# Weight units behind the last factors, and a first product between the two last of one bank, in a two-layer streaming encoder

## The chip, the cores and the metric

The kernel runs on one core of a Trainium2 chip. Its time is the device time of one execution in microseconds. A core has TensorE (PE; its weight loads are shown apart as PEld), VectorE (DVE), ScalarE (ACT), GpSimd (POOL) and SyncE (SP), which issues transfers. Each engine works through its own queue of instructions in order, and semaphores tie the queues together. Before the change three runs took 1084.51 to 1087.21 us, with a median of 1086.31.

## The reference

One step of an encoder with two layers, over 512 new frames of one stream and 64 of a running one, 576 columns together. Layer 0 mixes the frames by pooling, layer 1 by attention over selected keys. Behind each mixer stands a squared-ReLU MLP of 1024 to 4096 to 1024:

```python
def _mlp(h, w_up, w_down):
    u = jax.nn.relu(h @ w_up)
    return (u * u) @ w_down

for i in range(DEPTH):
    h = _rmsnorm(x, norm_mix[i])
    ...
    x = x + y.astype(x.dtype)
    x = x + _mlp(_rmsnorm(x, norm_mlp[i]), mlp_w_up[i], mlp_w_down[i]).astype(x.dtype)
return (_rmsnorm(x, norm_final), ...)
```

## The kernel before

**Numbers.** A float32 product is made of three products of a shorter format: every operand is split into a high part (a cast) and a low part (the rest). For weights this is a *unit*: L181 on ScalarE casts a raw 128x512 tile to `wh`, L182 on VectorE subtracts to get `wl`. For activations L470 on ScalarE and L473 on VectorE do the same, into `u`.

**Seven products.** In the MLP a block of two by two tiles is multiplied with seven products in place of eight (Strassen). `seven()` runs one such task. It uses three PSUM banks, `a`, `b` and `c`, and takes seven factors in this order: b11 into `b`, t1 into `c`, t2 into `b`, b21 into `a`, t3 into `b`, b22 into `c`, t4 into `b`. Behind the first product ScalarE copies `b` to `a` (L530). Each product is 12 matmuls of 128x288 (L501): four rows of the inner dimension, three matmuls each (wh with u's high part, wh with its low part, wl with the high part). Some weight units are sums of tiles, made on VectorE (L260, L264) from tiles that transfers have loaded and added to.

**Tasks.** An MLP is four chunks c of the inner width. Chunk 0 takes its up projection with plain products (L305). In c = 1, 2, 3, four up tasks `Up(c, j)` make four rows of activations (`u`, in L501's rows as `u_...`), then four down tasks `Down(q)` multiply them with the down weights and add to the residual x (L559). The fourth up task (j = 3) is *final*: its row is the last that the down tasks need. The first down task behind it is *late*: it runs rows 0 to 2 of its products first and row 3 behind them. This place is called a border here. There are six, at about 186, 277, 369, 834, 926 and 1017 us of the profiled execution.

**The final row.** An up task reads its banks with `lo0`, `hi1`, `hi0` and `lo1` while its last products still run. `hi1` adds a copy kept from bank `c` (`snap`) to bank `b` (L609), behind t3 and ahead of t4, which goes on to add into the same bank. L592 takes the ReLU times the norm's factor, L451 squares; L481, L484, L485 and L488 form the differences for t1, t2, t3 and t4 (the tile v, index 2, 3, 1, 0); `parts_of` splits them. In the last border of layer 1 the row's b12 part is also parked in PSUM (L494) and split later (L292) for the program's end.

**Order.** Nothing of this order is written by hand: a scheduler of the framework simulates the program and sets each engine's queue from the data's dependencies and its own estimates, in the order of the program where it has no reason for another. `ahead()` makes the next weight units, up to five ahead (`LEAD`), at the places where it is called, so the casts, subtractions and sums of later weights stand between the operations of the row. A raw tile is free for the next load (L213, on SyncE) once its unit is made, and GpSimd's queue adds a second tile to some of them in flight (L217, L238).

Of the kernel before, what the change touches and what calls it, by code (L numbers as in the profile page):

```python
# [12 lines left out]
ALU = mybir.AluOpType  # L13
# [9 lines left out]
HT = T // 2  # L23
# [33 lines left out]
def pool_dsa_kernel(ctx: ExitStack, tc: tile.TileContext, a, o):  # L57
    nc = tc.nc
    act, dve, pool, pe = nc.scalar, nc.vector, nc.gpsimd, nc.tensor
# [48 lines left out]
    def psum1(s="po"):  # L108
        return phase["po"].tile([P, 512], F32, tag="po", name=uid(s))

    def f32(t):
        return t.bitcast(F32)
# [156 lines left out]
    units = made()  # L269
# [18 lines left out]
    def split(dst, src, scale=None, sub=dve):  # L288

        if scale is None:  # L290
            act.copy(dst[:, 0], src)
            sub.tensor_tensor(dst[:, 1], src, f32(dst[:, 0]), ALU.subtract)  # L292
        else:
            act.activation(dst[:, 0], src, AF.Copy, scale=scale)
            dve.scalar_tensor_tensor(dst[:, 1], src, scale, f32(dst[:, 0]), ALU.mult, ALU.subtract)
# [101 lines left out]
    def mlp(layer, gi, late=0, end=None):  # L397
# [19 lines left out]
        parked = []  # L417
        rows = (0, 1, 2, 3)
# [48 lines left out]
                    phase["u"].tile([P, 7, 2, HT], F32R, tag="u", bufs=4, name=uid("u")))  # L467

        def upper(u, v, f):
            act.copy(u[:, f, 0], v[:, f])  # L470

        def lower(u, v, f):
            dve.tensor_tensor(u[:, f, 1], v[:, f], f32(u[:, f, 0]), ALU.subtract)  # L473

        def parts_of(u, v, f):

            upper(u, v, f)
            lower(u, v, f)

        def first_sum(v):  # L480
            dve.tensor_tensor(v[:, 2], v[:, 4], v[:, 1], ALU.subtract)  # L481

        def middle_sums(v):
            dve.scalar_tensor_tensor(v[:, 3], v[:, 5], -1.0, v[:, 2], ALU.mult, ALU.subtract)  # L484
            dve.tensor_tensor(v[:, 1], v[:, 5], v[:, 1], ALU.subtract)  # L485

        def last_sum(v):
            dve.scalar_tensor_tensor(v[:, 0], v[:, 6], -1.0, v[:, 3], ALU.mult, ALU.subtract)  # L488

        def left_over(j, b12):  # L490

            if j % 2 == 0:
                parked.append(psum("rest"))
            act.copy(parked[-1][:, j % 2, :HT], b12)  # L494

        def product(bank, w, operand, factor, js, first=False):
            for j in js:
                wh, wl = (t[:, j * P:(j + 1) * P] for t in w)
                uh, ul = (operand(j, factor, part) for part in range(2))
                for i, (wt, ut) in enumerate(((wh, uh), (wh, ul), (wl, uh))):  # L500
                    pe.matmul(bank[:, :HT], wt, ut, start=first and j == 0 and i == 0, stop=j == 3 and i == 2,  # L501
                              skip_group_check=True)

        tasks = [0]

        def ahead(n=1):

            how["sub"] = dve
            for _ in range(n):
                if len(ready) < LEAD:  # L510
                    u = next(units, None)
                    if u is not None:
                        ready.append(u)

        def take():
            if not ready:
                ahead()
            return ready.pop(0)

        def seven(operand, late, on):  # L520


            b, a_, c = (psum1(t) for t in "bac")
            on.banks = [t[:, :HT] for t in (a_, b, c)]
            w = take()
            product(b, w, operand, "b11", rows, True)
            tasks[0] += 1
            if tasks[0] <= SEEDED:
                pe.matmul(a_[:, :HT], w[0][:, :P], operand(0, "b11", 0), start=True, stop=True, skip_group_check=True)
            act.copy(a_[:, :HT], b[:, :HT])  # L530
            ahead()
            w1 = take()
            if late:
                w2 = take()
                product(c, w1, operand, "t1", rows[:3], True)
                product(b, w2, operand, "t2", rows[:3])
                product(c, w1, operand, "t1", rows[3:])
                on.c()
                ahead()
                product(b, w2, operand, "t2", rows[3:])  # L540
            else:
                product(c, w1, operand, "t1", rows, True)
                on.c()
                ahead()
                product(b, take(), operand, "t2", rows)
            on.b()
            ahead()
            for bank, factor, then in ((a_, "b21", on.lo0), (b, "t3", on.hi1), (c, "b22", on.hi0), (b, "t4", on.lo1)):
                product(bank, take(), operand, factor, rows)
                then()  # L550

        class Down:


            def __init__(self, q):
                self.lo, self.hi = ([x[2 * q + i][:, c0:c0 + HT] for i in range(2)] for c0 in (HT, 0))

            def update(self, to, bank, op):
                dve.tensor_tensor(to, to, self.banks[bank], op)  # L559

            def c(self):
                self.update(self.hi[1], 2, ALU.subtract)

            def b(self):
                self.update(self.hi[0], 1, ALU.add)
# [9 lines left out]
            def hi0(self):  # L575
                self.update(self.hi[0], 2, ALU.add)
                ahead()

            def lo1(self):
                self.update(self.lo[1], 1, ALU.subtract)  # L580
                ahead()

        class Up:


            def __init__(self, c, j):
                self.at, self.final = (c, j), j == half - 1
# [25 lines left out]
            def hi0(self):  # L613
                v = self.v
                dve.tensor_tensor(v[:, 1], self.banks[2], snap[:, 1], ALU.add)
                self.relu(1, v[:, 1], ALU.max, 0)
                if end and self.at[0] == 3:
                    left_over(self.at[1], v[:, 1])
                parts_of(self.u, v, slice(5 if self.final else 4, 6))
                first_sum(v)  # L620
                middle_sums(v)

            def lo1(self):
                v = self.v
                self.relu(6, self.banks[1], ALU.min, 1)
                if not self.final:
                    ahead()
                parts_of(self.u, v, slice(1, 4))
                last_sum(v)
                if not self.final:  # L630
                    ahead()
                parts_of(self.u, v, slice(0, 7, 6))
                if self.final:
                    ahead(2)

        def spread():

# [36 lines left out]
        for i in range(KT):  # L674
            w = next_block()
# [38 lines left out]
        if end:  # L714
            rest = []
            for j in range(half):
                if j % 2 == 0:
                    t = x_sums_tile()
                rest.append(t[:, j % 2])
                split(rest[j], parked[j // 2][:, j % 2, :HT])  # L720
            b11, b22, b21 = ([u[:, FACTORS.index(f)] for u in us] for f in ("b11", "b22", "b21"))
            end([rest + b22, b11 + b21])

# [856 lines left out]
```

## Time and profile before

| | |
|---|---|
| median of three runs | 1086.31 us (1084.51 to 1087.21) |
| the profiled execution | 1086.18 us |
| its span, first to last instruction | 1084.4 us |
| mean granted TensorE clock | 0.994 |
| weight casts L181 from raw tiles | 316, 194.8 us of ScalarE |
| weight subtractions L182 from raw tiles | 294, 206.1 us of VectorE |
| activations' low parts L473 | 100, 81.7 us of VectorE |
| activations' casts L470 | 100, 72.6 us of ScalarE |

A row of the profile names a line, an engine, an operation and its tiles as output<-input with their shapes. A number in brackets is the idle time of the engine just before the row, and what ended it. The span is what the trace covers; 1.8 us of the profiled execution lie around it.

### The profile page before, as it was taken

The page shows a single profiled execution, that of the slowest core. Times are in us where ns is not written, and L with a number is a line of the kernel's source. Part 1 is how long each engine was busy: PE and PEld are TensorE (multiplying, and loading weights), DVE is VectorE, ACT ScalarE, POOL GpSimd, SP SyncE. Part 2 cuts the span into 40 slices and gives each one's busy share as a digit, 9 for nine tenths or more (in the row PEclk, how much of TensorE's full clock was granted, in tenths as well). Part 3 has the DMA queues.
Part 4 walks back from the last instruction along what each step waited for, and adds up shares of the span by engine and source line. Part 5 has one row for each costly group of instructions (what it writes and reads, how often), then busy time and mean ns, then how long its engine had stood idle before and what let it go on. Part 6 is the DMA issues. An engine that isn't in the chain of part 4 may idle for free.

```text
span 1084.4 us, 21653 instructions
## 1 busy us (share of the span) xinstructions
PE 1052.2 (97%) x7942; PEld 1024.4 (94%) x7942; DVE 905.4 (83%) x1837; ACT 627.7 (58%) x1240; POOL 263.9 (24%) x285
## 2 busy tenths in 40 slices
PE   9999999999999999999989999999999999999996
PEld 8999999999999999999979888999999999999895
DVE  7889889879978987869998944689889879979974
ACT  8556457447546654444477776456467447547641
POOL 3200111111111100227687892000111111111001
PEclk9999999999999999999999999999999999999998
DMA  8233776676676654456642454443775776676512
GB/s 252 91 100 89 173 163 160 162 164 165 154 165 166 156 161 165 126 155 186 200 113 66 136 161 127 126 108 89 175 162 150 172 167 164 152 170 157 128 50 88
DMA packets 94460, 157.66 MB, mean 145 GB/s; under 512 B 13730, under 2 KB 25297, under 8 KB 94353
## 3 DMA queue, kind: packets, MB, share of 16 engines
q1 hardware_dynamic: 68720, 109.80, 33.1%
q0 software_dynamic: 15840, 28.84, 17.4%
q10 hardware_dynamic: 9792, 17.63, 5.3%
q8 instruction: 62, 1.02, 0.4%
q14 instruction: 46, 0.37, 0.1%
HBM read 141.15 MB, written 10.89 MB: 140 GB/s over the span
## 4 chain that ended last, share of the span: by engine, by line
PE 78%; DVE 8%; DMA 4%; ACT 3%; issue 3%; POOL 2%; SPq 1%; DVEq 0%; POOLq 0%; ACTq 0%
PE b L501 29%; PE c L501 15%; PE up L305 9%; PE a L501 7%; PE pj L305 5%; PE wo L305 2%; PE wa L305 2%; DVE wl L182 2%; PE pb L1005 1%; PE pt L1304 1%; PE sc L1278 1%; PE o L1336 1%; PE dn L305 1%; DMA raw<-in_w_in 1%; DMA raw<-in_w_down 1%
## 5 line engine op out<-in xcount | busy, mean ns | idle before, releaser
L181 ACT CAST wh<-raw 128x512 fp32r<-128x512 f32 (+1 forms) x316 | 194.8, 620 | 250.8 <-PE b L501 84.4
L182 DVE TENSOR_TENSOR wl<-raw,wh 128x512 fp32r<-128x512 f32 (+1 forms) x294 | 206.1, 703 | 38.6 <-ACT wh L181 29.2
L501 PE MATMUL b<-u,wh 128*128 128x288 f32 x992 | 202.2, 296 | 3.6 <-ACT a L530 3.2
L501 PEld LDWEIGHTS b<-u,wh 128*128 128x128 f32 x992 | 159.0, 188 | 6.0 <-ACT a L530 6.0
L181 ACT CAST wh<-sum 128x512 fp32r<-128x512 f32 x165 | 101.7, 620 | 81.3 <-PE b L501 42.3
L501 PE MATMUL b<-u,wl 128*128 128x288 f32 x496 | 145.3, 295 | 0.0
L182 DVE TENSOR_TENSOR wl<-sum,wh 128x512 fp32r<-128x512 f32 x165 | 111.9, 687 | 26.3 <-ACT wh L181 24.0
L238 POOL DMA_DIRECT2D sum<-in_w_down x31 | 27.1, 891 | 329.0 <-DVE u L473 119.3
L501 PE MATMUL c<-u,wh 128*128 128x288 f32 x496 | 102.8, 296 | 0.1
L501 PEld LDWEIGHTS b<-u,wl 128*128 128x128 f32 x496 | 92.9, 188 | 0.0
L305 PE MATMUL up<-xs,wh 128*128 128x288 f32 x512 | 89.6, 296 | 0.9 <-DVE x L1471 0.8
L501 PE MATMUL b<-xt,wh 128*128 128x288 f32 x384 | 78.2, 297 | 6.7 <-DVE v L609 6.7
L473 DVE TENSOR_TENSOR u<-v,u 128x864 fp32r<-128x864 f32 (+2 forms) x100 | 81.7, 824 | 0.5 <-ACT u L470 0.5
L501 PEld LDWEIGHTS c<-u,wh 128*128 128x128 f32 x496 | 79.9, 188 | 1.3 <-DVE x L559 1.3
L501 PE MATMUL b<-xs,wh 128*128 128x288 f32 x384 | 77.2, 294 | 0.0
L305 PEld LDWEIGHTS up<-xs,wh 128*128 128x128 f32 x512 | 74.6, 188 | 2.0 <-ACT wh L181 1.0
L470 ACT CAST u<-v 128x864 fp32r<-128x864 f32 (+2 forms) x100 | 72.6, 729 | 4.3 <-DVE v L488 3.4
L501 PE MATMUL c<-u,wl 128*128 128x288 f32 x248 | 73.1, 295 | 0.0
L238 POOL DMA_DIRECT2D sum<-in_w_up x24 | 20.7, 863 | 211.5 <-DVE wl L182 120.5
L501 PEld LDWEIGHTS b<-xt,wh 128*128 128x128 f32 x384 | 61.5, 188 | 8.1 <-DVE v L609 8.1
L305 PE MATMUL pj<-xs,wh 128*128 128x288 f32 x352 | 61.3, 295 | 0.0
L501 PEld LDWEIGHTS b<-xs,wh 128*128 128x128 f32 x384 | 61.2, 188 | 0.0
(289 smaller groups left out, 2722.3 us busy)
## 6 DMA issues: line engine op xcount, KB each, us to landing
raw<-in_w_up SPq DMA_DIRECT2D x128, 256.0 KB, 3.0
raw<-in_w_down SPq DMA_DIRECT2D x128, 256.0 KB, 2.9
raw<-in_w_o ACTq DMA_DIRECT2D x32, 256.0 KB, 3.1
sum<-in_w_down SPq DMA_DIRECT2D x31, 256.0 KB, 2.8
sum<-in_w_down POOLq DMA_DIRECT2D x31, 256.0 KB, 4.8
raw<-in_w_down POOLq DMA_DIRECT2D x31, 256.0 KB, 5.1
raw<-in_w_in ACTq DMA_DIRECT2D x30, 256.0 KB, 3.4
sum<-in_w_up SPq DMA_DIRECT2D x24, 256.0 KB, 2.9
```

The costliest lines, as they stand in the source:

```text
L181: act.copy(h, src)
L182: how["sub"].tensor_tensor(l, src, f32(h), ALU.subtract)
L238: pool.dma_start(s1, odd[:, 512:], accum_op=ALU.add)
L305: pe.matmul(pt[h][:, :m] if isinstance(pt, tuple) else pt[:, h, :m], wt, xs[k][:, part, c:c + m], start=(k == 0 and i == 0), stop=(k == n ...
L470: act.copy(u[:, f, 0], v[:, f])
L473: dve.tensor_tensor(u[:, f, 1], v[:, f], f32(u[:, f, 0]), ALU.subtract)
L501: pe.matmul(bank[:, :HT], wt, ut, start=first and j == 0 and i == 0, stop=j == 3 and i == 2, skip_group_check=True)
L1005: pe.matmul(pt[:, c0:c0 + rhs.shape[1]], lhs, rhs, start=n == 0, stop=n == len(steps) - 1)
L1278: pe.matmul(pt[:, hh, :nw], q[:, 2 * s + hh], ks[g][:, part, :nw], start=part == 0, stop=part == 1)
L1304: pe.transpose(pp[:, c:c + P], pr[:, hh, kt * P:(kt + 1) * P], ident)
L1336: pe.matmul(o[64 * hh:64 * hh + 64, s * P:(s + 1) * P], V[:, kt, vs], pT[:, c:c + P], start=kt == 0, stop=kt == i)
```

## The change

At the six borders it does four things. In the final up task only the parts of t1, t2 and b21 are cut at once; the differences for t3 and t4 and their parts are put off (`rest()`) until the next down task has updated x from bank `c`. Weight units are issued behind given instructions (`gates`): behind the final row's factors and later also behind that first update; a sum of weights (L260) is part of the unit. The first product of the next task (b11) is ordered behind the t3 product of the final up task, and that of the second down task behind the first one's b22 (`parted`). And in the last border the parked parts are split behind the same instructions (`kept`). The calls of `on.b()` and `ahead()` change places with the second part of t2's product only for a late task. Matmuls are the same in number; each border has one cast and one subtraction more, since a piece of three factors is cut in two.

```diff
         def middle_sums(v):
+            middle_sum(v)
+            side_sum(v)
+
+        def middle_sum(v):
             dve.scalar_tensor_tensor(v[:, 3], v[:, 5], -1.0, v[:, 2], ALU.mult, ALU.subtract)
+
+        def side_sum(v):
             dve.tensor_tensor(v[:, 1], v[:, 5], v[:, 1], ALU.subtract)
...
+        parted = []
+        gates = []
+        left = []
+        kept = []
+
+        @contextmanager
+        def behind(instructions):
+
+            with ExitStack() as st:
+                for ins in instructions:
+                    st.enter_context(tc.issue_after(ins))
+                yield
 
         def ahead(n=1):
...
-                    u = next(units, None)
+                    with behind(gates):
+                        u = next(units, None)
...
-            product(b, w, operand, "b11", rows, True)
+            with behind([parted.pop()] if parted else []):
+                product(b, w, operand, "b11", rows, True)
...
-                on.c()
+                first = on.c()
                 ahead()
                 product(b, w2, operand, "t2", rows[3:])
+                on.b()
+                if left:
+                    with tc.issue_after(first.ins):
+                        left.pop().rest()
+                    gates.append(first.ins)
+                    kept[:] = gates
+                ahead()
...
-                product(bank, take(), operand, factor, rows)
+                ins = product(bank, take(), operand, factor, rows)
+                if factor == "t3" and on.final or factor == "b22" and late and gates:
+                    parted.append(ins.ins)
                 then()
+            if late:
+                gates.clear()
...
+            def rest(self):
+                side_sum(self.v)
+                last_sum(self.v)
+                parts_of(self.u, self.v, slice(0, 2))
...
-                middle_sums(v)
+                middle_sum(v)
+                if not self.final:
+                    side_sum(v)
...
-                if not self.final:
-                    ahead()
+                if self.final:
+                    casts = [upper(self.u, v, f).ins for f in (slice(2, 4), slice(6, 7))]
+                    factors = lower(self.u, v, slice(2, 4))
+                    lower(self.u, v, slice(6, 7))
+                    ahead(2)
+                    gates[:] = [factors.ins, *casts]
+                    left.append(self)
+                    return
+                ahead()
...
-                split(rest[j], parked[j // 2][:, j % 2, :HT])
+                with behind(kept):
+                    split(rest[j], parked[j // 2][:, j % 2, :HT])
```

What that does to the queues is shown at the border at 277 us, where the row `v_2326` is made. TensorE before: the first product of the down task (bank `b_2483`), the final up task's t3 (`xs_...` into `b_2328`) and the start of its t4 (`xt_...`):

```order
L501 MATMUL b_2483<-u_2172,wh_2403 128x288 x2
L501 MATMUL b_2483<-u_2172,wl_2404 128x288
L501 MATMUL b_2328<-xs_642,wh_2344 128x288 x2
L501 MATMUL b_2328<-xs_642,wl_2345 128x288
L501 MATMUL b_2328<-xs_645,wh_2344 128x288 x2
L501 MATMUL b_2328<-xs_645,wl_2345 128x288
L501 MATMUL b_2328<-xs_648,wh_2344 128x288 x2
L501 MATMUL b_2328<-xs_648,wl_2345 128x288
L501 MATMUL b_2328<-xs_651,wh_2344 128x288 x2
L501 MATMUL b_2328<-xs_651,wl_2345 128x288
L501 MATMUL b_2328<-xt_983,wh_2380 128x288 x2
L501 MATMUL b_2328<-xt_983,wl_2381 128x288
```

The same place now, where the down task's bank is `b_2481`:

```order
L507 MATMUL b_2328<-xs_648,wh_2344 128x288 x2
L507 MATMUL b_2328<-xs_648,wl_2345 128x288
L507 MATMUL b_2328<-xs_651,wh_2344 128x288 x2
L507 MATMUL b_2328<-xs_651,wl_2345 128x288
L507 MATMUL b_2481<-u_1862,wh_2403 128x288 x2
L507 MATMUL b_2481<-u_1862,wl_2404 128x288
L507 MATMUL b_2481<-u_2017,wh_2403 128x288 x2
L507 MATMUL b_2481<-u_2017,wl_2404 128x288
L507 MATMUL b_2481<-u_2172,wh_2403 128x288 x2
L507 MATMUL b_2481<-u_2172,wl_2404 128x288
L507 MATMUL b_2328<-xt_983,wh_2380 128x288 x2
L507 MATMUL b_2328<-xt_983,wl_2381 128x288
```

The two rows of each of the three u tiles of b11 have moved behind t3; t4 follows them.

VectorE before, around the read of bank b (L609):

```order
L473 TENSOR_TENSOR u_2172<-v_2171,u_2172 128x2x288
L260 TENSOR_TENSOR sum_2555<-sum_2321,raw_2319 128x512
L182 TENSOR_TENSOR wl_2474<-raw_2193,wh_2473 128x512
L264 TENSOR_TENSOR sum_2401<-sum_2401,raw_2193 128x512
L592 SCALAR_TENSOR_TENSOR v_2326<-a_2329,rbm_149_866 128x288
L615 TENSOR_TENSOR v_2326<-c_2330,snap_982 128x288
L609 TENSOR_TENSOR v_2326<-b_2328,snap_982 128x288
L182 TENSOR_TENSOR wl_2500<-raw_2229,wh_2499 128x512
L592 SCALAR_TENSOR_TENSOR v_2326<-v_2326,rbm_149_866 128x288 x2
L473 TENSOR_TENSOR u_2327<-v_2326,u_2327 128x288
L481 TENSOR_TENSOR v_2326<-v_2326 128x288
L592 SCALAR_TENSOR_TENSOR v_2326<-b_2328,rbm_149_866 128x288
```

And now, where line 609 has become 648, 592 has become 631, 615 has become 654, and the differences L481, L484, L485, L488 are L481, L488, L491, L494:

```order
L473 TENSOR_TENSOR u_2172<-v_2171,u_2172 128x2x288
L182 TENSOR_TENSOR wl_2472<-raw_2193,wh_2471 128x512
L264 TENSOR_TENSOR sum_2401<-sum_2401,raw_2193 128x512
L631 SCALAR_TENSOR_TENSOR v_2326<-a_2329,rbm_149_866 128x288
L654 TENSOR_TENSOR v_2326<-c_2330,snap_982 128x288
L648 TENSOR_TENSOR v_2326<-b_2328,snap_982 128x288
L631 SCALAR_TENSOR_TENSOR v_2326<-v_2326,rbm_149_866 128x288 x2
L473 TENSOR_TENSOR u_2327<-v_2326,u_2327 128x288
L481 TENSOR_TENSOR v_2326<-v_2326 128x288
L488 SCALAR_TENSOR_TENSOR v_2326<-v_2326 128x288
L473 TENSOR_TENSOR u_2327<-v_2326,u_2327 128x288
L631 SCALAR_TENSOR_TENSOR v_2326<-b_2328,rbm_149_866 128x288
```

L260 and the unit of `wl_2500` are gone from between; the middle difference (L488) comes directly behind the first. A little further on VectorE's queue now reads, with L593 the update of x (L559 before):

```order
L182 TENSOR_TENSOR wl_2498<-raw_2229,wh_2497 128x512
L182 TENSOR_TENSOR wl_2526<-sum_2401,wh_2525 128x512
L593 TENSOR_TENSOR x_81<-x_81,c_2483 128x288
L491 TENSOR_TENSOR v_2326<-v_2326 128x288
L494 SCALAR_TENSOR_TENSOR v_2326<-v_2326 128x288
L182 TENSOR_TENSOR wl_2538<-raw_2252,wh_2537 128x512
L593 TENSOR_TENSOR x_81<-x_81,b_2481 128x288
L260 TENSOR_TENSOR sum_2557<-sum_2321,raw_2319 128x512
L182 TENSOR_TENSOR wl_2560<-raw_2319,wh_2559 128x512
L593 TENSOR_TENSOR x_81<-x_81,a_2482 128x288
L182 TENSOR_TENSOR wl_2579<-sum_2321,wh_2578 128x512
L473 TENSOR_TENSOR u_2327<-v_2326,u_2327 128x2x288
```

The put-off differences L491 and L494, the units and L260 stand behind or between the updates, and the parts of t3 and t4 (L473 of 128x2x288) at its end.

ScalarE before, around the copy of bank b (L530), in the same border:

```order
L470 CAST u_2327<-v_2326 128x288
L451 ACTIVATE v_2326<-v_2326 128x288 x2
L181 CAST wh_2527<-sum_2401 128x512
L470 CAST u_2327<-v_2326 128x288
L181 CAST wh_2535<-raw_2252 128x512
L530 COPY a_2484<-b_2483 128x288
L451 ACTIVATE v_2326<-v_2326 128x288
L470 CAST u_2327<-v_2326 128x3x288
L470 CAST u_2327<-v_2326 128x2x288
```

And now, with the copy at L551:

```order
L451 ACTIVATE v_2326<-v_2326 128x288 x2
L470 CAST u_2327<-v_2326 128x288
L470 CAST u_2327<-v_2326 128x2x288
L551 COPY a_2482<-b_2481 128x288
L451 ACTIVATE v_2326<-v_2326 128x288
L470 CAST u_2327<-v_2326 128x288
L181 CAST wh_2497<-raw_2229 128x512
L181 CAST wh_2525<-sum_2401 128x512
L181 CAST wh_2537<-raw_2252 128x512
```

The two weight casts ahead of the copy (`wh_2527`, `wh_2535`) stand behind the factors now, and t1 and t2 (128x2x288) are cast ahead of it.

More of the change, by code (lines that the diff above doesn't have):

```diff
@@ L469, in upper @@
         def upper(u, v, f):
-            act.copy(u[:, f, 0], v[:, f])
+            return act.copy(u[:, f, 0], v[:, f])
         def lower(u, v, f):
-            dve.tensor_tensor(u[:, f, 1], v[:, f], f32(u[:, f, 0]), ALU.subtract)
+            return dve.tensor_tensor(u[:, f, 1], v[:, f], f32(u[:, f, 0]), ALU.subtract)
         def parts_of(u, v, f):
             upper(u, v, f)
-            lower(u, v, f)
+            return lower(u, v, f)
         def first_sum(v):
@@ L500, in product @@
                 for i, (wt, ut) in enumerate(((wh, uh), (wh, ul), (wl, uh))):
-                    pe.matmul(bank[:, :HT], wt, ut, start=first and j == 0 and i == 0, stop=j == 3 and i == 2,
-                              skip_group_check=True)
+                    ins = pe.matmul(bank[:, :HT], wt, ut, start=first and j == 0 and i == 0, stop=j == 3 and i == 2,
+                                    skip_group_check=True)
+            return ins
         tasks = [0]
+        parted = []
[8 more added lines that the diff above has]
+                yield
         def ahead(n=1):
@@ L545, in seven @@
                 product(b, take(), operand, "t2", rows)
-            on.b()
-            ahead()
+                on.b()
+                ahead()
             for bank, factor, then in ((a_, "b21", on.lo0), (b, "t3", on.hi1), (c, "b22", on.hi0), (b, "t4", on.lo1)):
-                product(bank, take(), operand, factor, rows)
+                ins = product(bank, take(), operand, factor, rows)
+                if factor == "t3" and on.final or factor == "b22" and late and gates:
+                    parted.append(ins.ins)
                 then()
+            if late:
+                gates.clear()
         class Down:
+            final = False
             def __init__(self, q):
@@ L558, in update @@
             def update(self, to, bank, op):
-                dve.tensor_tensor(to, to, self.banks[bank], op)
+                return dve.tensor_tensor(to, to, self.banks[bank], op)
             def c(self):
-                self.update(self.hi[1], 2, ALU.subtract)
+                return self.update(self.hi[1], 2, ALU.subtract)
             def b(self):
@@ L625, in lo1 @@
                 self.relu(6, self.banks[1], ALU.min, 1)
-                if not self.final:
-                    ahead()
+                if self.final:
[6 more added lines that the diff above has]
+                    return
+                ahead()
                 parts_of(self.u, v, slice(1, 4))
                 last_sum(v)
-                if not self.final:
-                    ahead()
+                ahead()
                 parts_of(self.u, v, slice(0, 7, 6))
-                if self.final:
-                    ahead(2)
         def spread():
```

## The prediction

> **What bounds the kernel now.** I read the page first.
>
> ```profile
> PE 1052.2 (97%) x7942; PEld 1024.4 (94%) x7942; DVE 905.4 (83%) x1837; ACT 627.7 (58%) x1240; POOL 263.9 (24%) x285
> PE 78%; DVE 8%; DMA 4%; ACT 3%; issue 3%; POOL 2%; SPq 1%; DVEq 0%; POOLq 0%; ACTq 0%
> ```
>
> TensorE is busy 97% of the span and carries 78% of the chain that ended last. The change leaves the number of matmuls as it is, so it can gain only where TensorE waits. The list of waits of TensorE names those places in the MLP's seven products (L501).
>
> ```profile
> PE b L501 <- DVE v L609: 6.7, 6, 1.2
> PE b L501 <- ACT a L530: 3.2, 7, 1.0
> ```
>
> Total us, number of waits, longest. Six waits for L609 are the six borders where an up stage ends and a down stage begins. I looked at one of them, at 277 us, engine by engine. Rows give start, duration, and in brackets the idle time ahead of them with what ended it.
>
> ```profile
> 277.09 0.29 PE L501 MATMUL b<-xs,wl 128*128 128x288 f32 x1
> 278.53 0.53 PE L501 MATMUL b<-xt,wh 128*128 128x288 f32 x2 [1.15 <-DVE v L609]
> 280.23 0.43 PE L501 MATMUL b<-u,wh 128*128 128x288 f32 x2
> 280.63 0.43 PE L501 MATMUL c<-u,wh 128*128 128x288 f32 x2
> 281.68 0.29 PE L501 MATMUL c<-u,wl 128*128 128x288 f32 x1
> 282.12 0.53 PE L501 MATMUL b<-u,wh 128*128 128x288 f32 x2
> 285.14 0.29 PE L501 MATMUL c<-u,wl 128*128 128x288 f32 x1
> 285.67 0.29 PE L501 MATMUL a<-u,wl 128*128 128x288 f32 x1
> 285.99 0.53 PE L501 MATMUL c<-u,wh 128*128 128x288 f32 x2
> ```
>
> Nine matmuls of t1 start between 280.63 and 281.68: a pitch of 1.05/8 = 0.13 us when nothing waits. From the last of t3 (277.09) to the first of t4 (278.53) pass 1.44, so 1.31 are lost; t4's twelve then take 1.70 where twelve pitches are 1.59, so a restart costs 0.1 more. Ahead of t2 (281.68 to 282.12) 0.31 are lost and ahead of b22 (285.67 to 285.99) 0.19, each with its restart. That is about 2.1 us a border. What holds TensorE is VectorE's queue:
>
> ```profile
> 274.82 0.76 DVE L473 TENSOR_TENSOR u<-v,u 128x576 fp32r<-128x576 f32 x1
> 275.49 0.69 DVE L260 TENSOR_TENSOR sum<-sum,raw 128x512 f32<-128x512 f32 x1
> 276.09 0.69 DVE L182 TENSOR_TENSOR wl<-raw,wh 128x512 fp32r<-128x512 f32 x1
> 276.69 0.69 DVE L264 TENSOR_TENSOR sum<-sum,raw 128x512 f32<-128x512 f32 x1
> 277.30 0.45 DVE L592 SCALAR_TENSOR_TENSOR v<-a,rbm 128x288 f32<-128x288 f32 x1
> 277.66 0.45 DVE L615 TENSOR_TENSOR v<-c,snap 128x288 f32<-128x288 f32 x1
> 278.03 0.45 DVE L609 TENSOR_TENSOR v<-b,snap 128x288 f32<-128x288 f32 x1
> 278.39 0.68 DVE L182 TENSOR_TENSOR wl<-raw,wh 128x512 fp32r<-128x512 f32 x1
> 278.99 0.82 DVE L592 SCALAR_TENSOR_TENSOR v<-v,rbm 128x288 f32<-128x288 f32 x2
> 283.51 1.72 DVE L473 TENSOR_TENSOR u<-v,u 128x864 fp32r<-128x864 f32 x2
> 285.48 0.46 DVE L559 TENSOR_TENSOR x<-x,c 128x288 f32<-128x288 f32 x1 [0.24 <-PE c L501]
> ```
>
> No row from 274.82 to 278.39 has a bracket: VectorE runs without pause. t3's last matmul ends at 277.38, but L609, which reads its bank, starts at 278.03, straight behind L615. So **L609 waits for its own queue, not for t3**. Starts lie 0.37 us apart for 288 columns, 0.60 for 512, 0.67 for 576; TensorE starts 0.50 behind L609 (278.03 to 278.53) and 0.51 behind L559.
>
> **The change part by part, at an ordinary border.**
>
> *The first product of the next task goes between t3 and t4 of one bank.* Nine matmuls, 9 x 0.13 = 1.2 us, move behind t3. t3 ends 1.2 earlier, and t4 could start no later than now. Since L609 waits for VectorE's queue, this part alone gains nothing: TensorE asks for t4 at the same 277.2 and waits as before. It would be worth up to 1.2 only if VectorE were ahead.
>
> *The weight sum L260 leaves the queue ahead of L609.* One 128x512 operation, 0.60. L182 then starts at 275.49, L264 at 276.09, L592 at 276.70, L615 at 277.06, L609 at 277.42, and t4 at 277.92: **0.60 gained**. t4's wait stays, with 0.70.
>
> *Weight units behind the factors, and t1, t2, b21 cut first.* From here I work the new order forward with the same spacings. TensorE: t4 from 277.92 to 279.62 (1.70), the last row of b11 to 280.02, t1 and one matmul more (10) to 281.34. The copy of bank b (L530 before) is what t2 waits for:
>
> ```profile
> 279.48 0.81 ACT L451 ACTIVATE v<-v 128x288 f32<-128x288 f32 x2 [0.73 <-DVE v L592]
> 281.15 0.62 ACT L181 CAST wh<-raw 128x512 fp32r<-128x512 f32 x1
> 281.68 0.39 ACT L530 COPY a<-b 128x288 f32<-128x288 f32 x1
> ```
>
> A weight cast stands straight ahead of it (0.53 from start to start), and another one a little before; both go behind. On VectorE two L592 follow L609 at 277.79, the first low part at 278.53, and the first and middle sums at 278.90 and 279.27. ScalarE follows VectorE by 0.49 (278.99 to 279.48), so its cast of t1 and t2 starts at 279.76; 576 columns take 0.53 x 576/512 = 0.60, and the copy runs at 280.36. t2 starts 0.44 behind the copy (281.68 to 282.12): 280.80, while TensorE is busy until 281.34. **This wait, 0.31 and its 0.1, goes.** t2 (10), b21 (9) and the seven left-over matmuls of the last row end their issue at 281.34 + 26 x 0.1325 = 284.79. The last of bank c is the second of those seven and ends near 284.28; VectorE's update of x by c follows at 284.33 (before, 285.14 + 0.29 and then 285.48), and b22 0.51 behind it: 284.84. Before it was 285.99. **1.15 a border is gained**, and 0.05 and a restart of the last wait stay.
>
> VectorE makes it in time: low parts of t1 and t2 at 280.48, of b21 at 281.6, two L182 at 282.15 and 282.75, free by 283.4 for the update at 284.33.
>
> *What is put off.* The sums of t3 and t4, their two parts, L260 and two L182 now come behind that update. They are no less work; the factor parts even cost one instruction more, 0.67 + 0.37 + 0.76 = 1.80 on VectorE where two take 1.72 now. Starts: 284.70, 285.07 (sums), 285.44 L182, 286.04 update, 286.41 L260, 287.01 L182, 287.6 update, 287.97 L182, and the parts of t4 and t3 from 288.58 to 289.34. TensorE wants the last row's low part of t3 after b22 (to 286.54) and 22 matmuls, at 289.45. **The margin is 0.1 us**, so I cost the debt at nothing, and at up to 0.7 (one L182 or L260 in the way, and a restart) if that cover is gone. The low part of the weights for the second task is ready at 287.70 and wanted at 288.13.
>
> *Loads.* Two raw tiles are now freed 3.7 and 2.9 us later, since their L182 move from 278.39 and 282.54 to 282.15 and 285.44. SyncE issues its loads in one queue, and GpSimd adds to what they bring.
>
> ```profile
> 283.25 8.71 SPq L213 DMA_DIRECT2D raw<-in_w_down  x4
> 286.64 0.86 POOL L217 DMA_DIRECT2D raw<-in_w_down  x1 [0.36 <-DVE x L559]
> raw<-in_w_down POOLq DMA_DIRECT2D x31, 256.0 KB, 5.1
> 300.48 0.62 ACT L181 CAST wh<-raw 128x512 fp32r<-128x512 f32 x1 [0.95 <-PE b L501]
> ```
>
> The raw tile loaded first at 283.25 is added to at 286.64, lands at 291.7, and is cast at 300.48: 8.7 us of slack against 2.9. I cost it at nothing.
>
> *The last border (1017 us)* also holds four splits of the parked bank, L292:
>
> ```profile
> 1018.24 0.54 PE L501 MATMUL b<-xt,wh 128*128 128x288 f32 x2 [1.07 <-DVE v L609]
> 1019.81 0.45 DVE L292 TENSOR_TENSOR xt<-rest,xt 128x288 fp32r<-128x288 f32 x1
> 1022.67 0.53 PE L501 MATMUL b<-u,wh 128*128 128x288 f32 x2 [0.99 <-ACT a L530]
> 1025.76 0.40 PE L501 MATMUL a<-u,wh 128*128 128x288 f32 x1 [0.17 <-ACT u L470]
> 1027.06 0.41 PE L501 MATMUL a<-u,wh 128*128 128x288 f32 x1 [0.23 <-DVE u L473]
> ```
>
> TensorE idles 1.07 + 0.99 + 0.17 + 0.23 = 2.46 here, and VectorE has no pause for 16 us (windows, below). So only what leaves the path helps: the four L292, 4 x 0.37 = 1.5, which are now behind the first update and which no product of the down stage reads. I take 1.5, with 0 and 2.46 as ends.
>
> *Side effect.* The scheduler also orders some rows of layer 1's attention otherwise, from about 553 to 640 us. No work is added there. I take nothing, and bound it by the waits that stand there now (rivals).
>
> **Sum.** Five borders at 1.15 and one at 1.5: 7.25 us. The profiled execution took 1086.18 (span 1084.4), 0.13 below the median of 1086.31. 1086.18 - 7.25 = **1078.9 us**.
>
> **Rivals.**
>
> *The debt comes back.* If the put-off parts come 0.6 to 0.7 late at every border, each ordinary one keeps 0.45 and the last 1.5: 3.75 in all, **1082.4**. For it: a margin of 0.1 and a VectorE without pause. Against: 0.24 of idle stands ahead of L559 now.
>
> *VectorE gets ahead of TensorE.* If L609's queue is shorter than I work out, the new place of b11 hides the rest of t4's wait, 0.70 + 0.1 at six borders: 4.8 more, **1074.1**. Against it: no pause in the rows above.
>
> *The change doesn't do what it says:* t4 waits as before because only TensorE's order moved, and L260 is missed elsewhere. Only t2's 0.41 goes at six borders: 2.5, **1083.7**, no measurable change.
>
> *Slower: the attention rows and the clock.* The windows:
>
> ```profile
> 273.00:289.00 16.00, 14.69 (x107) 13.98 (x106) 15.76 (x32) 9.88 (x19) 2.59 (x3) 1.00 0.57 135
> 560.00:566.00 6.00, 2.92 (x20) 2.21 (x19) 5.86 (x19) 1.92 (x8) 3.94 (x4) 1.00 0.48 131
> 566.00:574.00 8.00, 7.58 (x40) 7.37 (x39) 5.65 (x22) 4.55 (x16) 5.32 (x4) 0.57 0.13 35
> 1013.00:1029.00 16.00, 13.54 (x95) 12.54 (x94) 16.00 (x34) 10.56 (x23) 1.26 (x2) 1.00 0.42 97
> ```
>
> Columns: stretch, length, busy time of PE, PEld, DVE, ACT and POOL, granted clock, DMA share, GB/s. At the borders the clock stays at 1.00. From 560 to 566 TensorE works 2.92 of 6 us, and for the next 8 us the clock is 0.57. Such an event costs the 3.1 us idle and 0.43 x 8 = 3.4, 6.5 together. If the new order of these rows makes one event more, the time is 1078.9 + 6.5 = **1085.4**, no change; two more make **1091.9**, slower. [...] For it: VectorE works 5.86 of the 6 us, so an order there is easily worse. Against: the same work in nearly the same order. If the present event goes, the gain grows by up to 6.5, to 1072.4.
>
> [...]
>
> **How the numbers follow.** Forecast 1078.9 (own range 1076.5 to 1081.4): 0.50. Debt, 1082.4: 0.16, a third of it beyond 1083. VectorE ahead, 1074.1: 0.10. Nothing but t2, 1083.7: 0.05. One more clock event: 0.08; two, or another loss of that size: 0.06. The present event gone: 0.05. A measurement of this kernel tells about 0.3% from no change, so faster means below 1083.0 and slower above 1089.6. Faster 0.50 + 0.11 + 0.10 + 0.05 = 0.76; same 0.05 + 0.05 + 0.08 = 0.18; slower 0.06. The range runs from 1074.0 to 1085.5; the clock cases beyond it hold some 0.11.
>
> **What would show it.** In the profile after: L648 (L609 before) directly behind L654 with no idle, and t4's wait near 0.6 (the list: about 3.6 us in six); no wait of b for the copy L551 at these borders, against 3.2 now; b22's update within 0.3 us of bank c's last matmul; no new wait for L473 at t3. The forecast fails if L473 or L182 appears among TensorE's waits, or if the windows around 560 show another clock.

## The result, and the profile after

The changed kernel takes 1078.55 us (median of six runs, 1077.58 to 1080.68); the kernel before took 1086.28 beside it. The ratio is 0.9934, with a 95% interval of 0.9919 to 0.9949: 7.7 us faster. The profiled execution took 1078.55, with a span of 1076.8 where it was 1084.4.

The lines of the changed kernel's page that answer to those shown of before:

```profile
PE 1049.3 (97%) x7942; PEld 1022.2 (95%) x7942; DVE 904.3 (84%) x1843; ACT 628.5 (58%) x1246; POOL 263.6 (24%) x285
PE 79%; DVE 11%; DMA 4%; issue 3%; ACT 1%; POOL 1%; SPq 0%; DVEq 0%; POOLq 0%; ACTq 0%
```

And of its list of TensorE's waits (total us, times, longest):

```profile
PE b L507 <- DVE v L648: 3.1, 6, 0.5
PE b L507 <- ACT a L551: 1.9, 4, 0.5
PE b L507 <- DVE u L473: 0.4, 1, 0.4
PE b L507 <- DVE wl L182: 0.4, 1, 0.4
```

The wait for L648 (L609 before) still stands at all six borders, but with 3.1 us in place of 6.7. The copy (L551, L530 before) is waited for four times, not seven: those four lie in chunk 0 (two in each layer), which the change leaves alone. The waits for L473 and L182 are new and both lie in the last border. The border at 277 us again in TensorE's rows (start, duration, idle time and its releaser):

```profile
276.25 0.29 PE L507 MATMUL b<-u,wl 128*128 128x288 f32 x1
277.06 0.53 PE L507 MATMUL b<-xt,wh 128*128 128x288 f32 x2 [0.52 <-DVE v L648]
280.48 0.43 PE L507 MATMUL b<-u,wh 128*128 128x288 f32 x2
283.81 0.29 PE L507 MATMUL a<-u,wl 128*128 128x288 f32 x1
284.08 0.50 PE L507 MATMUL c<-u,wh 128*128 128x288 f32 x2
288.52 0.30 PE L507 MATMUL b<-u,wl 128*128 128x288 f32 x1
288.66 0.29 PE L507 MATMUL b<-u,wh 128*128 128x288 f32 x1
```

Ahead of t4, 0.68 us are lost (277.06 - 276.25 - 0.13) where it was 1.31. t2 starts at 280.48 without a wait. Ahead of b22 (284.08) 0.14 are lost, where it was 0.19. And t3 takes the put-off low part at 288.66, one pitch behind the matmul before it. VectorE's queue at the same place:

```profile
273.96 0.75 DVE L473 TENSOR_TENSOR u<-v,u 128x576 fp32r<-128x576 f32 x1
274.63 0.68 DVE L182 TENSOR_TENSOR wl<-raw,wh 128x512 fp32r<-128x512 f32 x1
275.23 0.68 DVE L264 TENSOR_TENSOR sum<-sum,raw 128x512 f32<-128x512 f32 x1
275.83 0.45 DVE L631 SCALAR_TENSOR_TENSOR v<-a,rbm 128x288 f32<-128x288 f32 x1
276.20 0.44 DVE L654 TENSOR_TENSOR v<-c,snap 128x288 f32<-128x288 f32 x1
276.56 0.44 DVE L648 TENSOR_TENSOR v<-b,snap 128x288 f32<-128x288 f32 x1
280.92 0.46 DVE L473 TENSOR_TENSOR u<-v,u 128x288 fp32r<-128x288 f32 x1 [0.38 <-ACT u L470]
283.48 0.45 DVE L593 TENSOR_TENSOR x<-x,c 128x288 f32<-128x288 f32 x1 [0.74 <-PE c L507]
287.72 0.75 DVE L473 TENSOR_TENSOR u<-v,u 128x576 fp32r<-128x576 f32 x1
```

No row from 273.96 to 276.56 has a bracket: L648 still waits for the queue ahead of it, which is now shorter by L260. Behind it VectorE has two pauses ahead of the update, 0.38 and 0.74, where it had one of 0.24 before.

**Where the 7.6 us of the span came from.** Both traces hold 7942 matmuls, and at the limits used below the same product stands under the same number, so the stages can be timed by the starts of the same matmuls: the MLP of layer 0 from the 1201st to the 2901st, that of layer 1 from the 6001st to the 7801st, and the reordered part of the attention from the 3901st to the 4421st.

| us | MLP 0 (3 borders) | MLP 1, to the 7401st (2 borders) | last border | MLPs | between the MLPs | of it attention rows |
|---|---|---|---|---|---|---|
| before | 232.28 | 190.02 | 56.90 | 479.2 | 409.9 | 72.4 |
| after | 229.33 | 188.28 | 55.87 | 473.5 | 407.8 | 70.8 |
| gain | 2.95 | 1.74 | 1.03 | 5.7 | 2.1 | 1.6 |

The MLPs gave 5.7 us and the stretch between them 2.1. (The rest of the span lost 0.2.) **The total is the one forecast; its parts are not**, and the experiments were chosen for that.

### The profile page after: what moved, and what is told of

Its sections match the earlier page's. It is cut to its first block, busy times and chain, and to the rows that moved or that the text cites. A ratio compares the mean times of both kernels' runs of the same rounds, so it can differ in the third digit from the quotient of the medians.

```text
span 1076.8 us, 21654 instructions
## 1 busy us (share of the span) xinstructions
PE 1049.3 (97%) x7942; PEld 1022.2 (95%) x7942; DVE 904.3 (84%) x1843; ACT 628.5 (58%) x1246; POOL 263.6 (24%) x285
## 4 chain that ended last, share of the span: by engine, by line
PE 79%; DVE 11%; DMA 4%; issue 3%; ACT 1%; POOL 1%; SPq 0%; DVEq 0%; POOLq 0%; ACTq 0%
PE b L507 30%; PE c L507 16%; PE up L305 9%; PE a L507 8%; PE pj L305 3%; DVE wl L182 2%; PE wa L305 2%; PE pt L1350 1%; PE sc L1324 1%; PE o L1382 1%; PE pb L1051 1%; PE dn L305 1%; DVE work L1277 1%; DMA raw<-in_w_down 1%; DVE m L1276 1%
## 5 line engine op out<-in xcount | busy, mean ns | idle before, releaser
L182 DVE TENSOR_TENSOR wl<-raw,wh 128x512 fp32r<-128x512 f32 (+1 forms) x294 | 205.4, 701 | 38.4 <-ACT wh L181 33.8
L182 DVE TENSOR_TENSOR wl<-sum,wh 128x512 fp32r<-128x512 f32 x165 | 112.3, 686 | 22.3 <-ACT wh L181 20.8
L473 DVE TENSOR_TENSOR u<-v,u 128x576 fp32r<-128x576 f32 (+3 forms) x106 | 83.1, 786 | 2.8 <-ACT u L470 2.8
L470 ACT CAST u<-v 128x576 fp32r<-128x576 f32 (+3 forms) x106 | 73.9, 699 | 5.6 <-DVE v L494 2.3
L507 PE MATMUL c<-u,wl 128*128 128x288 f32 x248 | 73.2, 295 | 0.0
L451 ACT ACTIVATE v<-v 128x288 f32<-128x288 f32 (+1 forms) x112 | 51.8, 476 | 18.0 <-DVE v L631 14.3
```

The costliest lines, as they stand in the source:

```text
L182: how["sub"].tensor_tensor(l, src, f32(h), ALU.subtract)
L451: act.activation(v, v, AF.Square)
L470: return act.copy(u[:, f, 0], v[:, f])
L473: return dve.tensor_tensor(u[:, f, 1], v[:, f], f32(u[:, f, 0]), ALU.subtract)
L507: ins = pe.matmul(bank[:, :HT], wt, ut, start=first and j == 0 and i == 0, stop=j == 3 and i == 2, skip_group_check=True)
```

## The experiments

Theory A is that of the prediction: at t4 TensorE waits for VectorE's queue, so what leaves that queue is gained, and the place of b11 is worth nothing by itself. Theory B: TensorE lacked work between t3 and t4, and b11 fills the gap. Two more questions are whether the gain between the MLPs belongs to the change, and whether the last border gains as forecast.

**1. The kernel before once more**, without any edit.

> The kernel before once more, for its profile alone. The question is the stretch between the two MLPs (from 411 to 755 us before, 343.5 us), which the changed kernel passes in 341.3. If that gain belongs to the order of the attention rows, this execution takes 343.5 again (within 0.5) and shows the clock of 0.57 behind the waits at 560 us again. If the clock differs from one execution to the next, it takes up to 3.4 us less in this one, with the clock at 1.00. At the borders: the same waits ahead of t4 as before, 1.23 to 1.31 us.

It took 1086.27. MLPs 479.1, between them 409.9, the attention rows 72.6: as in the first profile, within 0.2. The clock fell behind the waits at 560 us again (0.74 over 560 to 580 us, 0.83 in the first).

**2. Only the place of b11** (that of the first down task; the change also places the second one's, behind b22). The main lines of the edit, in the kernel before:

```diff
-            product(b, w, operand, "b11", rows, True)
+            with behind([parted.pop()] if parted else []):
+                product(b, w, operand, "b11", rows, True)
...
+                ins = product(bank, take(), operand, factor, rows)
+                if factor == "t3" and on.final:
+                    parted.append(ins.ins)
```

> The kernel before with one part of the change: the first product b11 of the down stage stands between t3 and t4. VectorE's and ScalarE's queues are as before. Theory A (L609 waits for VectorE's own queue): the wait ahead of t4 stays at 1.2 to 1.3 us at all six borders, and the time is that of before, 1086.2, within 0.1%. Theory B (TensorE lacked work between t3 and t4): the wait falls by the nine matmuls, 1.2 us a border, 7 us in all, to 1079.

1086.64 against 1086.65, ratio 1.0002 (0.9993 to 1.0011); MLPs 479.2. Its list of waits has one line for t4:

```profile
PE b L501 <- DVE v L623: 6.6, 6, 1.1
```

Rows of VectorE and TensorE at the second border, in order of time:

```profile
275.36 0.69 DVE L260 TENSOR_TENSOR sum<-sum,raw 128x512 f32<-128x512 f32 x1
...
277.54 0.45 DVE L629 TENSOR_TENSOR v<-c,snap 128x288 f32<-128x288 f32 x1
277.90 0.45 DVE L623 TENSOR_TENSOR v<-b,snap 128x288 f32<-128x288 f32 x1
278.40 0.53 PE L501 MATMUL b<-xt,wh 128*128 128x288 f32 x2 [1.07 <-DVE v L623]
```

t3 ends 1.2 us earlier and nothing comes of it: L623 (L609) starts straight behind L629 as before, and t4 0.50 behind it. Theory B is out.

**3. The change without the place of b11.** The lines that fill `parted` are left out:

```diff
-                if factor == "t3" and on.final or factor == "b22" and late and gates:
-                    parted.append(ins.ins)
```

> The change without the part that places b11: TensorE's order of b11, t3 and t4 is as before, VectorE's queue as in the changed kernel. Theory A: L609 comes 0.6 us earlier all the same, t4 waits 0.65 to 0.7 us, and the time is that of the changed kernel, 1078.6, within 0.2%. Theory B: most of the gain goes, the wait ahead of t4 is above 1.2 us, and the time is 1082 to 1086.

1078.89, ratio 0.9931 (0.9916 to 0.9946). MLPs 473.8, so the place of b11 is worth 0.3 us of the change's 5.7. The idle time ahead of t4 is 0.55 here and 0.52 with it. Its rows of VectorE and TensorE:

```profile
276.47 0.45 DVE L652 TENSOR_TENSOR v<-c,snap 128x288 f32<-128x288 f32 x1
276.85 0.46 DVE L646 TENSOR_TENSOR v<-b,snap 128x288 f32<-128x288 f32 x1
277.37 0.53 PE L507 MATMUL b<-xt,wh 128*128 128x288 f32 x2 [0.55 <-DVE v L646]
```

L646 follows the last L473 ahead of it by 2.62 us (from 274.23), where L623 in experiment 2 took 3.21 (from 274.69): 0.59 less, by L260, though TensorE's order is that of before. (t3's last matmul starts at 276.52 here, 0.33 ahead of L646; experiment 9 comes back to this.)

**4. The change without gates**: units and sums are not held behind the factors.

```diff
-                    with behind(gates):
-                        u = next(units, None)
+                    u = next(units, None)
```

> The change with the weight units not held behind the factors; the parts of t3 and t4 are still put off and b11 still stands between t3 and t4. L260 is back in the queue ahead of L609. Theory A: the wait ahead of t4 is 1.2 to 1.3 us again, so 0.6 us a border are lost; the waits ahead of t2 and b22 still gain something because two sums fewer stand ahead of the factors. In all 2 to 4 us of the 5.7 that the MLPs gain go: 1081 to 1083. Theory B: the wait ahead of t4 stays at 0.7 and the time at 1079.

1086.01, ratio 0.9995 (0.9986 to 1.0005): no change from before. The direction was theory A's, the size was not: I expected 2 to 4 us to go and 5.0 of 5.7 went (MLPs 478.5; what is left is 1.0 at the last border). The wait ahead of t4 is back, by its list of waits:

```profile
PE b L507 <- DVE v L647: 6.8, 6, 1.2
```

And so is the one ahead of t2, by ScalarE's rows at the second border:

```profile
280.49 0.62 ACT L181 CAST wh<-sum 128x512 fp32r<-128x512 f32 x1
...
281.35 0.62 ACT L181 CAST wh<-raw 128x512 fp32r<-128x512 f32 x1
281.88 0.39 ACT L550 COPY a<-b 128x288 f32<-128x288 f32 x1
```

Both casts stand ahead of the copy again. Fewer sums ahead of the factors did nothing for it.

**5. Only the sum gated**: as 4, but L260 alone is held.

```diff
-            dve.tensor_tensor(s2, s1, a11, ALU.add)
+            with ExitStack() as st:
+                for ins in how.get('gates', ()):
+                    st.enter_context(tc.issue_after(ins))
+                dve.tensor_tensor(s2, s1, a11, ALU.add)
...
+            how['gates'] = gates
```

> The change with only the weight sum L260 held behind the factors; the units' casts and subtractions are not held, as in the run without gates. If L260 alone is what t4 waits for, the wait ahead of t4 falls from 1.27 us to about 0.7 at all borders, while the wait ahead of t2 (0.30 and a restart of 0.1) and the one ahead of b22 (0.18 and 0.1) stay, since the two casts still stand ahead of the copy. The ordinary borders then gain 0.6 of the change's 1.0 each, and the MLPs together about 3.6 us more than without gates. If the units' subtractions matter at t4 too, the wait stays near 1.2.

1080.5, ratio 0.9949 (0.9934 to 0.9964). MLPs 475.8, 2.7 less than without gates where I expected 3.6: 0.52 at each of the five ordinary borders ((232.45 - 230.81 + 190.12 - 189.16) / 5, from experiment 4 and here) and 0.08 at the last. The wait ahead of t4 falls as expected (0.67 lost at the second border), those ahead of t2 (0.31) and b22 (0.17) stay. At the last border the 0.6 gained at t4 came back as a wait of 0.71 for L182.

**6. Without putting t3 and t4 off**: `rest()` is called at once.

```diff
-                if left:
-                    with tc.issue_after(first.ins):
-                        left.pop().rest()
+                if gates:
...
+                    self.rest()
                     ahead(2)
                     gates[:] = [factors.ins, *casts]
-                    left.append(self)
```

> The change without the part that puts t3 and t4 off: their two sums and their parts are issued at once, behind the other factors; units, sums and b11 stand as in the changed kernel. Theory A (VectorE's queue ahead of each read): t4 waits 0.65 to 0.7 as in the changed kernel, since nothing ahead of L609 differs. Two sums more (0.73) stand ahead of the update of x by bank c; VectorE idles 0.38 + 0.74 there in the changed kernel, so b22 waits at most 0.1 longer, and the time is within 0.2% of the changed kernel's. Rival (putting off is what the change lives by): 0.7 us a border come back, 4 us, to 1083.

1079.68, ratio 0.9940 (0.9925 to 0.9955). MLPs 474.3: putting off is worth 0.8 us in all, nearer to theory A's "nothing" than to 4 us. At an ordinary border it is worth 0.2, and at the last one it costs 0.3 (55.58 there, 55.87 in the changed kernel). The 0.2 come at a place that I had not named: the next update of x, which L473, L182 and L260 now separate from the first (2.24 us from start to start at the second border, 1.71 in the changed kernel); TensorE loses 0.22 and a restart behind it.

**7. The splits not held** at the last border (`kept`):

```diff
-                with behind(kept):
+                with behind([]):
                     split(rest[j], parked[j // 2][:, j % 2, :HT])
```

> The change without holding back the four splits of the parked bank (L292) at the last border. They stand between the factors again. If holding them is what this border gains, its gain of 1.0 us goes and waits ahead of t2 or b22 stand there again. If they only move work from one stretch without pause to the next, TensorE's new waits for L182 and L473 behind b22 (0.52 and 0.56 now) shrink by what comes back ahead of t2 and b22, and the border takes the same within 0.3 us. The other five borders and the attention stage are as in the changed kernel.

Its one execution took 1077.87. The last border takes 54.90 where the changed kernel takes 55.87: **holding the splits costs 1.0 us**, where both of my expectations had it gain or be neutral. The two lists of TensorE's rows with an idle time at that border, of the changed kernel first, then without the hold:

```profile
1011.01 0.53 PE L507 MATMUL b<-xt,wh 128*128 128x288 f32 x2 [0.49 <-DVE v L648]
1021.79 0.40 PE L507 MATMUL b<-u,wl 128*128 128x288 f32 x1 [0.36 <-DVE wl L182]
1023.79 0.40 PE L507 MATMUL b<-u,wh 128*128 128x288 f32 x1 [0.40 <-DVE u L473]
```

```profile
1011.34 0.53 PE L507 MATMUL b<-xt,wh 128*128 128x288 f32 x2 [0.49 <-DVE v L648]
```

VectorE behind the update in the changed kernel:

```profile
1020.69 0.45 DVE L292 TENSOR_TENSOR xt<-rest,xt 128x288 fp32r<-128x288 f32 x1
1021.05 0.68 DVE L182 TENSOR_TENSOR wl<-raw,wh 128x512 fp32r<-128x512 f32 x1
...
1022.02 0.45 DVE L292 TENSOR_TENSOR xt<-rest,xt 128x288 fp32r<-128x288 f32 x1
...
1022.99 0.75 DVE L473 TENSOR_TENSOR u<-v,u 128x576 fp32r<-128x576 f32 x1
```

And VectorE without the hold:

```profile
1014.14 0.81 DVE L292 TENSOR_TENSOR xt<-rest,xt 128x288 fp32r<-128x288 f32 x2
1014.96 0.76 DVE L473 TENSOR_TENSOR u<-v,u 128x576 fp32r<-128x576 f32 x1
1015.64 0.45 DVE L292 TENSOR_TENSOR xt<-rest,xt 128x288 fp32r<-128x288 f32 x1
...
1017.05 0.68 DVE L182 TENSOR_TENSOR wl<-sum,wh 128x512 fp32r<-128x512 f32 x1
1017.73 0.46 DVE L593 TENSOR_TENSOR x<-x,c 128x288 f32<-128x288 f32 x1
```

The splits fill the pauses that VectorE has between the factors and the update (no bracket ahead of 1017.73); held back, one of them stands ahead of the L182 and two ahead of the L473 that TensorE then waits for, in a queue without pause. What TensorE loses ahead of these two matmuls falls from 0.52 and 0.57 to 0.16 and 0.20 without the hold: 0.73 of the 1.0.

**8 and 9. GpSimd makes L264 at the borders, with and without the place of b11.** A test of theory A by dose: one more operation leaves the queue ahead of L609.

```diff
-                    dve.tensor_tensor(s2, s2, a12, ALU.add)
+                    how.get('sum', dve).tensor_tensor(s2, s2, a12, ALU.add)
...
+            how['sum'] = pool if on.final else dve
...
+            how['sum'] = dve
```

> The change, and at the borders GpSimd makes the weight sum L264 that stands ahead of L609 on VectorE. Theory A: one 128x512 operation, 0.60, leaves the queue ahead of L609, and the wait ahead of t4 falls from 0.68 to 0.1 at all six borders: 3.5 us, 1075. Theory B (t4's wait is a fixed distance from t3 to t4): no change, 1078.6. The sum itself takes GpSimd about 1.3 us (its 128x512 subtractions take 1.29) and is wanted some 5 us later.

> The same with GpSimd's sum, without the part that places b11 between t3 and t4. Theory A: now t3's own end binds, since VectorE is ready for L609 before it. t4 waits about 0.6 to 0.7 as in the changed kernel, and the time is 1078 to 1079: GpSimd's sum gains nothing without the place of b11, and the place gains 3.5 us with it. Rival (the place of b11 is worth nothing whatever stands in VectorE's queue): the time is that of the kernel with GpSimd's sum and b11 between t3 and t4.

With b11's place 1075.84, ratio 0.9902 (0.9887 to 0.9917), MLPs 469.9: 3.6 us less than the changed kernel. Without it 1079.53, ratio 0.9938 (0.9921 to 0.9954), and MLPs 473.8, as in the changed kernel. The times differ from the changed kernel's by less (2.7 us gained) and by more (1.0 lost) than the MLPs do; with GpSimd's sum the attention rows stand in another order and take 72.5 and 72.9 us. Rows of VectorE and TensorE with b11's place, at the second border:

```profile
275.15 0.45 DVE L650 TENSOR_TENSOR v<-b,snap 128x288 f32<-128x288 f32 x1
275.44 0.29 PE L507 MATMUL b<-u,wl 128*128 128x288 f32 x1
275.65 0.53 PE L507 MATMUL b<-xt,wh 128*128 128x288 f32 x2
```

And without it, at the same border:

```profile
276.04 0.29 PE L507 MATMUL b<-xs,wl 128*128 128x288 f32 x1
276.38 0.46 DVE L648 TENSOR_TENSOR v<-b,snap 128x288 f32<-128x288 f32 x1 [0.55 <-PE b L507]
```

With the place of b11, t4 follows b11 with 0.08 lost, and L650 no longer stands in TensorE's list of waits. Without it, VectorE itself idles 0.55 ahead of L648 and starts it 0.34 behind the start of t3's last matmul: now t3 binds. In experiment 3 that distance was 0.33 already, though VectorE's queue had no pause: queue and t3 were ready together there. So the place of b11 gains nothing with a full queue ahead of L609 (experiment 2), 0.3 us in the change (3), and 3.9 us once the queue is short enough (473.8 - 469.9). Two limits stood within a few hundredths of a microsecond of each other, and each hid what the other's removal would bring.

**10. The changed kernel once more**, without any edit.

> The changed kernel once more, for its profile. With the splits not held the same attention rows ran at a clock of 0.83 from 560 to 580 us, and the stage took 48.65 us; the changed kernel's first profile had 1.00 there and 48.56. If the stage's time follows the order of its rows and not the clock, it takes 48.5 to 48.7 again, whichever clock it shows. If the clock decides, a clock of 1.00 goes with 48.6 and 0.83 with 50 or more.

This execution took 1083.13, the slowest of this kernel. MLPs 473.5, as in its first profile; attention rows 71.3; but 412.5 between the MLPs. From the 4061st matmul to the 4421st, the stretch that the expectation speaks of, it took 48.55, as forecast if the order decides (50.75 in the kernel before). From its list of waits:

```profile
PE up L305 <- DVE x L1517: 1.8, 1, 1.8
PE sc L1324 <- ACT rp L1141: 1.6, 1, 1.6
PE pj L305 <- DVE rp L1137: 1.3, 1, 1.3
```

The first profile has the first two with 1.1 each and not the third, so these three make up 2.5 of the 4.7 us. TensorE's order is the same, so such waits differ from one execution to the next.

**11 and 12. GpSimd's sum, with the splits not held, or held behind the second down task's update.**

> GpSimd's sum and b11 between t3 and t4 as above, and the four splits not held. If the two gains add, t4 waits below 0.1 at all borders and the last border loses another 1.0 us against GpSimd's sum alone, since TensorE's waits for L182 and L473 there shrink: 1075.8 - 1.0 = 1074.8. If GpSimd's sum has already used VectorE's idle time there, less than 0.3 remains.

> GpSimd's sum as above, and the four splits held behind the second down task's update in place of the first's. If the splits are what stands in the way of L182 and L473 behind b22, these waits (0.52 and 0.56) shrink to 0.15 and nothing, and the last border gains about 0.9 us, as much as with the splits not held: 1074.9. If the second L260 is what stands there, both waits stay.

MLPs 468.9 in both, with the last border at 54.3 where GpSimd's sum alone has 55.3: the two gains add. Both waits behind b22 shrink, to 0.16 and 0.20 lost, so the splits stood in the way; whether the second L260 that stands there accounts for what is left was not tried. The times, 1076.72 and 1077.45 where 1074.8 and 1074.9 were expected (ratios 0.9911, 0.9894 to 0.9929, and 0.9911, 0.9898 to 0.9925), can't be told from 1075.84: the stretch between the MLPs took 412.2, 409.7 and 409.5 in the three profiles, and that spread covers a gain of 1 us. By the MLPs these two are the best versions; by the times, GpSimd's sum (experiment 8) beats the change, with intervals that just miss each other, and the intervals of these two overlap with both.

## Why the prediction came out

**The place of b11: right.** Forecast at nothing; alone it is nothing (experiment 2), and in the change 0.3 us. That it would pay once VectorE is ahead was named as a rival, and experiment 8 made that case.

**L260 ahead of L609: right.** Forecast 0.60 a border; held alone it gives 0.52 (experiment 5).

**The waits ahead of t2 and b22: right in place, somewhat large.** The wait for the copy goes at all six borders. The chain worked out for VectorE stands in the trace step by step: L648 to t4 in 0.50, the low parts, the copy, the update behind the second of the seven left-over matmuls. Only b22 follows the update in 0.60 and not in 0.51 (283.48 to 284.08). An ordinary border gains (2.95 + 1.74) / 5 = 0.94, not 1.15. The rows of the second border show 1.07: from the last matmul ahead of t4 to the first of b22 it was 8.90 (277.09 to 285.99) and is 7.83. Where the rest goes was not followed up.

**The debt: right at the ordinary borders.** The forecast margin of 0.1 held: L473 ends at 288.47, the matmul that takes its part starts at 288.66, and there is no wait for L473. Putting off is worth 0.2 at such a border (experiment 6). The loads, also costed at nothing, made TensorE wait nowhere: the four lines of its list above are all of its waits in the seven products.

**The last border: the step was wrong, though the size is near.** Its gain was to be "the four L292, 4 x 0.37 = 1.5, which are now behind the first update". It gains 1.03, and holding the splits takes 1.0 from it (experiment 7). What I missed: the change gives VectorE pauses ahead of the update and none behind it, so work moved from the one side to the other leaves the pauses unused and makes the put-off work late. The debt that I had costed at nothing came due here, with waits of 0.36 and 0.40.

**The side effect in the attention: a term that I set to nothing and that gave 1.1 to 1.8.** Five profiles with the new order of TensorE's attention rows (after, and experiments 3, 5, 7, 10) have 70.8 to 71.3 us there, three with the old order (before, 1, 2) 72.4 to 73.2. So it belongs to the order. The other kernels have orders of their own: 70.4 us without putting off, 72.8 without gates, 72.2 to 73.0 with GpSimd's sum. VectorE pauses for 2.1 to 2.8 us of these rows with the new order and for 6.2 to 6.9 with the old; why this order is quicker was not tried. In the first profile after, it made up for the 1.5 us by which the borders fell short: 5 x 1.15 + 1.5 = 7.25 against 5.7.

**The signs, and luck.** Of what was to show the forecast, L648 directly behind L654, 3.1 us in six waits, and no wait for the copy at the borders came. But two signs by which it was to fail came as well: L182 and L473 among TensorE's waits, and another clock around 560 us. The first belongs to the 1.0 us that holding the splits costs, at one border alone; the second cost nothing that shows. The mechanism at the five ordinary borders was forecast. That the total came within 0.4 us of 1078.9 is luck: a step that was wrong and terms that were too large met a gain that was not in the sum.

**The clock rival: its price was wrong, and what brings such an event about was not shown.** I had 0.43 x 8 = 3.4 us for a stretch at a reduced clock. The windows from 560 to 580 us of the changed kernel, of experiment 7 and of experiment 10, in that order, which share the order of TensorE's rows (length, busy PE, PEld, DVE, ACT, POOL, clock, DMA share, GB/s):

```profile
560.00:580.00 20.00, 17.11 (x135) 15.01 (x135) 19.93 (x69) 14.82 (x46) 14.05 (x17) 1.00 0.21 54
```

```profile
560.00:580.00 20.00, 18.48 (x130) 17.27 (x132) 19.91 (x69) 15.05 (x46) 14.21 (x16) 0.83 0.20 54
```

```profile
560.00:580.00 20.00, 16.76 (x118) 15.29 (x117) 19.86 (x70) 13.80 (x42) 14.55 (x16) 0.91 0.31 85
```

The clock was 1.00, 0.83 and 0.91, and the attention rows took 70.8, 70.9 and 71.3. VectorE is busy for 19.9 of 20 us there, so a slower TensorE cost little or nothing. Nor does the order fix the clock, which differs among these three executions. In the changed kernel's first profile the event of before was gone, for which I had up to 6.5 us; the rows gained as much in experiment 7, where the clock was 0.83. Nor was it the idler TensorE that the lower clock followed: in the 20 us ahead of these windows, from 540 to 560 us, TensorE was busy for 18.56, 18.84 and 19.26 us, at a clock of 1.00 in all three.

## What to carry to other kernels

Before work is placed into a gap of one engine, look whether the engine that ends the gap starts its operation straight behind another of its own: then only its queue counts, and the filler is worth nothing until that queue is shorter than the gap (here nothing, experiment 2). Two limits that end within a few hundredths of a microsecond of each other must be moved together (here the place of b11 alone gave 0.3 us of the MLPs, GpSimd's sum alone nothing, both 3.9: experiments 3, 9 and 8). Work that is put off should go where the engine has pauses, not merely off the path, since behind the critical operation it may be the next to be late (here waits of 0.36 and 0.40 us at the last border).

## What the runs showed of the hardware

The group of GpSimd's sums in experiment 8 (busy us, mean ns of one, idle time before):

```profile
L264 POOL TENSOR_TENSOR sum<-sum,raw 128x512 f32<-128x512 f32 x6 | 14.1, 2346 | 7.7 <-DVE wl L182 7.7
```

GpSimd needs 2.35 us for the sum that takes VectorE 0.69 (L264 at 276.69 us before), where I had expected 1.3, the time of its subtractions of the same shape (L182, 1.29 us); what makes the difference was not tried. At the second border of the changed kernel a matmul that waits for VectorE started 0.50 us behind the start of a 128x288 operation at t4 (276.56 to 277.06) and 0.60 behind the update ahead of b22 (283.48 to 284.08). The stretch between the MLPs differed by up to 4.7 us between two executions of one kernel (407.8 and 412.5), while the MLPs repeated within 0.1 us (479.2 and 479.1 before, 473.5 twice after); a change inside them of a few tenths of a microsecond can be read from one trace and not from a few times.
